# Where three tiles' tap products stand in TensorE's order, and x's third and fourth tile in two transfers

## The chip, the cores and the metric

The kernel runs on one core of one Trainium2 chip. A core has five engines that each take their instructions in order: TensorE (PE in the profile, with its weight loads as PEld), VectorE (DVE), ScalarE (ACT), GpSimd (POOL) and SyncE (SP, which here only issues transfers). They wait for each other and for transfers through semaphores. The metric is device microseconds of one execution, lower is better.

## The reference

Two layers on x of 512 tokens by 1024 channels, float32. Layer 0 is a convolution module and a gated feed-forward part, layer 1 is sliding-window attention and another feed-forward part, and an RMS norm ends it. Only the head of layer 0 matters here:

```python
def rmsnorm(x, g):
    xf = x.astype(jnp.float32)
    xf = xf * lax.rsqrt(jnp.mean(xf * xf, axis=-1, keepdims=True) + EPS)
    return (xf * g.astype(jnp.float32)).astype(x.dtype)

def conformer_conv(x, w_pw1, b_pw1, w_dw, b_dw, ln_g, ln_b, w_pw2, b_pw2):
    a = jax.nn.glu(x @ w_pw1 + b_pw1, axis=-1)
    y = lax.conv_general_dilated(                # 31 causal taps, each channel for itself
        a, w_dw[:, None, :].astype(a.dtype), window_strides=(1,),
        padding=((CONV_WIDTH - 1, 0),), dimension_numbers=('NWC', 'WIO', 'NWC'),
        feature_group_count=D_MODEL) + b_dw
    y = jax.nn.silu(layernorm(y, ln_g, ln_b))
    return y @ w_pw2 + b_pw2
...
h = h + conformer_conv(rmsnorm(h, norm_mix[l]), ...)
h = h + swiglu_ffn(rmsnorm(h, norm_ffn[l]), ffn_w_up[l], ffn_w_down[l])
```

## The kernel before

Channels lie on the 128 partitions and tokens along the row, so x is eight tiles of 128 by 512 (`h[0]` to `h[7]`), loaded by `load_x` (L376). Every float32 product is taken apart into a rounded high part and the rest, and costs three matmuls (`mm3`, `mm3_in_turn`, L339): high by high, high by rest, rest by high. ACT rounds the high part, DVE subtracts it. Weights come as chunks of 128 by 1024; `advance` (L252) loads six chunks ahead and splits three ahead.

**The start.** `load_x(0, 1)`, `load_x(1, 2)`, the rest of the first weight chunk, `load_x(2, 4)`, the second chunk, `load_x(4, 6)`, `load_x(6, 8)` and the taps' table are issued by SP in that order (L379 to L386); ACT issues three small transfers beside them. The loop at L705 splits the x tiles in order, on ACT and on DVE, with the first two weight chunks in pieces between them; on DVE it also lays out the tables of tap weights behind tiles 1 and 3 (L715). Both orders are written out by hand (`acts`, `dves`). Then both engines form the sum of squares for the norm.

**The first stage** handles the eight channel tiles `ct` of the convolution one after the other (`Conv`, L735, loop at L945):

- `project`: two halves of eight steps; a step is one `mm3_in_turn`, so a projection is 48 matmuls. They fill two banks, `gt` (the gate's argument) and `lin`. In the second half, for every tile but the first, the four steps for `gt` come first and then the four for `lin`. After each step it calls `inside(ct)` with the half and the number of the step.
- `begin`: `gate` multiplies both by the norm's factor, takes the sigmoid, and writes the gated tile `apad` (DVE L766, L768, L769 with ACT L767 between). Then SP writes `apad` to DRAM (`rowsd`) and reads it back four times, shifted, into `shifted`, one read for each quarter of the partitions (L775, L777). `products` makes some taps on ACT (L822) with sums on POOL (L824); `taps` makes others on DVE, one instruction for each tap.
- `rounds` makes 12 to 20 of the 31 taps on TensorE, from `shifted` and the tables, into a bank of its own: three, four or five rounds of four 32-column matmuls (the trace records each as two). It needs all four shifted reads.
- `last` (DVE L841) adds that bank to the tile's other taps.

TensorE's order is a chain (`in_turn`, L335): whatever is called first runs first, and what waits holds all that follows. The other engines' order is laid out by the framework's planner when the kernel is built, in which a line called earlier goes ahead if its inputs are ready; only the chains `tapped`, `copies`, `acts` and `dves` are fixed. The program's transfers share eight landing semaphores in rotation, so a transfer is issued once the one eight places before it has landed.

The rounds of a tile are called by `inside` of a later projection: those of tile 0 at the end of projection 2 (L927), those of tiles 1, 2 and 3 inside projections 3, 4 and 5 (L930 to L932), those of tiles 4 to 6 behind projection 7 (L949), and those of tile 7 last, in two halves, for the layer norm's means (L960). At the end of projection 3 stands a small table product, of projection 4 `shift_rows`, of projections 5 and 6 `sums` of the finished tiles and their squares. Then come the layer norm, the second pointwise product, and the two layers' other parts, all on the same TensorE.

Of the kernel before, what the change touches and what calls it, by code (L numbers as in the profile page):

```python
# [21 lines left out]
KT = D // P  # L22
# [150 lines left out]
def hybrid_trunk(ctx: ExitStack, tc: tile.TileContext, xT, W, prm_in, wdw_in, rnd_in, sinks, relb, onehot, fin, out):  # L173
# [87 lines left out]
    def split_chunk(i):  # L261
        r = block(i) if PLAN[i][0] == "prod" else raws.pop(i)
        stream["split"] = i + 1
        hi = wpool.tile([P, 1024], F32R, tag="whi", name=uid("whi"))
        lo = wpool.tile([P, 1024], F32R, tag="wlo", name=uid("wlo"))
        with ExitStack() as hold:
            for ins in held[0]:
                hold.enter_context(tc.issue_after(ins))
            done = (nc.scalar.copy(hi, r).ins, lo_engine[0].tensor_sub(lo, r, f32(hi)).ins)  # L269
        splits[i] = (hi, lo)  # L270
        return done
# [104 lines left out]
    def load_x(a, b):  # L376
        nc.sync.dma_start(hT[:, a:b, :], xT[a:b].rearrange("k p s -> p k s"))
# [1 line left out]
    load_x(0, 1)  # L379
    load_x(1, 2)  # L380
    nc.sync.dma_start(early[0][0][:, 256:1024], W[0][:, 256:1024])
    load_x(2, 4)
    nc.sync.dma_start(early[1][0], W[1])
    load_x(4, 6)
    load_x(6, 8)
# [257 lines left out]
    with conv_stage:  # L643
# [15 lines left out]
        def table():  # L659
            pf = bank()  # L660
            fs = temp()[0:NH, 0:3 * P]
            nc.tensor.matmul(pf[0:NH, 0:3 * P], lhs, oh, start=True, stop=True)
            nc.scalar.mul(fs, pf[0:NH, 0:3 * P], -1.0)
            nc.scalar.mul(sk, sk, -1.0)
            nc.sync.dma_start(f1.rearrange("o (h k) -> (o h) k", h=NH), fs)

        def table_rows():
            nc.sync.dma_start(fd.rearrange("q h k -> q (h k)"), f1.to_broadcast([16, NH * 3 * P]))
# [28 lines left out]
        def round_weights(cts, after=None):  # L697
            for ct in cts:
                at, n = ROUND_COLS[ct], 4 * ROUNDS[ct]
                with tc.issue_after(after) if after is not None else nullcontext():  # L700
                    after = nc.vector.tensor_mul(weights_of[ct], eye.unsqueeze(1).to_broadcast([P, n, 32]),
                                                 rnd[:, at:at + n].unsqueeze(2).to_broadcast([P, n, 32])).ins
            return after
# [145 lines left out]
        def shift_rows():  # L849

            b = bank()
            for e in range(2):
                in_turn(b, ones_m, y[e], start=e == 0, stop=e == 1)
            nc.scalar.mul(shift, b, -1.0 / 256)
            for t in y[0:2]:
                nc.vector.tensor_add(t, t, shift)
            nc.gpsimd.tensor_add(y[2], y[2], shift)

        def sums(*cts):

            if st[0] is None:
                st[0] = bank()
            src = []
            for i in cts:
                sq = next_of(1, sqs)
                nc.scalar.square(sq, y[i])
                src += [y[i], sq]
            for n, t in enumerate(src):
                in_turn(st[0][n * 32:(n + 1) * 32, :], ones32, t, start=cts[0] == 0, stop=cts[0] == KT - 2 - n // 2 * 2)
# [44 lines left out]
        def inside(ct):  # L914
            def at(half, n):
                if ct == 1 and (half, n) == (0, 5):
                    rms0.step1()
                    round_weights((0, 1, 2, 3), rms0.had)
                if ct == 1 and (half, n) == (1, 1):
                    rms0.step2()  # L920
                    convs[0].gate()
                    split_limit[0] = 2 * KT
                    held[0] = (convs[0].gated,)
                    held[0] = (split_chunk(5)[1],)
                    convs[0].products()
                    convs[0].taps()
                if half == 1 and n == 7 and ct == 2:  # L927
                    convs[0].rounds()
                    convs[0].last()
                if half == 0 and n == 7 and 3 <= ct < KT - 2:  # L930
                    convs[ct - 2].rounds()
                    convs[ct - 2].last()  # L932
                if half == 1 and n == 7:
                    if ct == 3:
                        table()
                    if ct == 4:
                        table_rows()
                    if ct == 4:
                        shift_rows()
                    if ct in (5, 6):  # L940
                        sums(2 * ct - 10, 2 * ct - 9)
            return at
# [370 lines left out]
```

## Time and profile before

| what | value |
|---|---|
| median of 3 runs | 1056.72 us (1055.94 to 1058.72) |
| the profiled execution | 1053.6 us, its span 1051.8 us |
| granted TensorE clock, mean | 0.999 |
| DVE, ACT, POOL busy | 754.4 us (72%), 501.4 us (48%), 184.5 us (18%) |
| first stage, from the first product to the layer norm | about 5 to 147 us of the span |

The span runs from the first to the last instruction; the execution's time has 1.8 us around it. Times inside the profile are microseconds from the start of the span. In a timeline row stand start, duration, engine, line, operation, output and inputs, the number of instructions merged, and in brackets how long the engine stood idle before it and what ended that. A releaser is inferred from what ended last, so it can name a bystander. In the answer for a tile, "DMA to landing" is the time from a transfer's issue until its data is there.

### The profile page before, as it was taken

The page shows a single profiled execution, that of the slowest core. Times are in us where ns is not written, and L with a number is a line of the kernel's source. Part 1 is how long each engine was busy: PE and PEld are TensorE (multiplying, and loading weights), DVE is VectorE, ACT ScalarE, POOL GpSimd, SP SyncE. Part 2 cuts the span into 40 slices and gives each one's busy share as a digit, 9 for nine tenths or more (in the row PEclk, how much of TensorE's full clock was granted, in tenths as well). Part 3 has the DMA queues.
Part 4 walks back from the last instruction along what each step waited for, and adds up shares of the span by engine and source line. Part 5 has one row for each costly group of instructions (what it writes and reads, how often), then busy time and mean ns, then how long its engine had stood idle before and what let it go on. Part 6 is the DMA issues. An engine that isn't in the chain of part 4 may idle for free.

```text
span 1051.8 us, 16099 instructions
## 1 busy us (share of the span) xinstructions
PE 1037.6 (99%) x6492; PEld 899.4 (86%) x6492; DVE 754.4 (72%) x981; ACT 501.4 (48%) x765; POOL 184.5 (18%) x200
## 2 busy tenths in 40 slices
PE   9999999999999999999999999999999999999997
PEld 7666568888998999899879878788899988998996
DVE  8799857599776587576684677578977754776663
ACT  6666645352552355155453766345355432542443
POOL 0799801311000000000130534041100000000000
PEclk9999999999999999999999999999999999999999
DMA  7656675324244124221323120232323431342112
GB/s 256 179 160 180 148 139 120 100 80 141 81 124 138 63 98 160 61 81 62 120 81 100 61 61 22 80 105 87 131 98 105 140 118 41 109 145 88 41 61 80
DMA packets 36918, 111.64 MB, mean 106 GB/s; under 512 B 4395, under 2 KB 7260, under 8 KB 36828
## 3 DMA queue, kind: packets, MB, share of 16 engines
q1 hardware_dynamic: 35692, 109.32, 35.0%
q10 hardware_dynamic: 1152, 1.29, 0.4%
q8 instruction: 51, 0.84, 0.3%
q14 instruction: 23, 0.19, 0.1%
HBM read 106.25 MB, written 4.73 MB: 106 GB/s over the span
## 4 chain that ended last, share of the span: by engine, by line
PE 88%; DVE 2%; issue 1%; ACT 1%; POOL 0%; POOLq 0%; ACTq 0%
PE bank L346 23%; PE bank L345 23%; PE bank L347 23%; PE bank L337 18%; PE bank L1242 2%; DVE quad L459 1%; DVE wlo L269 1%; ACT whi L269 0%; PE bank L450 0%; PE bank L1232 0%; PE bank L433 0%; DVE h L488 0%; DVE quad L280 0%; POOL rr L908 0%; ACT tmp L280 0%
## 5 line engine op out<-in xcount | busy, mean ns | idle before, releaser
L346 PE MATMUL bank<-quad,whi 128*128 128x256 f32 (+1 forms) x1536 | 488.5, 320 | 1.3 <-DVE quad L459 0.9
L345 PE MATMUL bank<-quad,whi 128*128 128x256 f32 (+1 forms) x1536 | 483.9, 320 | 0.3 <-ACT tmp L606 0.3
L347 PE MATMUL bank<-quad,wlo 128*128 128x256 f32 (+1 forms) x1536 | 482.6, 320 | 0.0
L269 ACT CAST whi<-raw 128x1024 fp32r<-128x1024 f32 x174 | 182.5, 1050 | 294.8 <-PE bank L346 197.4
L346 PEld LDWEIGHTS bank<-quad,whi 128*128 128x128 f32 x1536 | 292.6, 190 | 22.8 <-DVE quad L459 1.3
L345 PEld LDWEIGHTS bank<-quad,whi 128*128 128x128 f32 x1536 | 291.3, 190 | 23.0 <-ACT quad L280 0.7
L347 PEld LDWEIGHTS bank<-quad,wlo 128*128 128x128 f32 x1536 | 290.0, 190 | 20.2
L269 DVE TENSOR_TENSOR wlo<-raw,whi 128x1024 fp32r<-128x1024 f32 x174 | 220.5, 1270 | 112.4 <-ACT whi L269 110.1
L337 PE MATMUL bank<-quad,whi 128*128 128x512 f32 x512 | 160.9, 395 | 0.6 <-ACT whi L280 0.6
L337 PEld LDWEIGHTS bank<-quad,whi 128*128 128x128 f32 x512 | 94.8, 188 | 26.7 <-issue 4.0
L269 DVE TENSOR_TENSOR wlo<-blocks,whi 128x1024 fp32r<-128x1024 f32 x54 | 65.5, 1221 | 57.5 <-ACT whi L269 57.5
L269 ACT CAST whi<-blocks 128x1024 fp32r<-128x1024 f32 x54 | 56.6, 1048 | 91.7 <-PE bank L346 69.4
L337 PE MATMUL bank<-quad,wlo 128*128 128x512 f32 x256 | 99.9, 390 | 0.1
L824 POOL TENSOR_TENSOR quad<-quad 128x512 f32<-128x512 f32 x53 | 76.4, 1442 | 10.9 <-ACT quad L822 7.8
L337 PEld LDWEIGHTS bank<-quad,wlo 128*128 128x128 f32 x256 | 48.1, 188 | 10.7 <-DVE wlo L280 0.4
L1253 POOL TENSOR_TENSOR rs<-ss,mhalf 128x1 f32<-128x1 f32 x4 | 2.2, 549 | 298.0 <-DVE ss L1251 298.0
L423 POOL TENSOR_TENSOR tmp<-tmp,tmp 128x512 f32<-128x512 f32 x21 | 32.9, 1568 | 111.8 <-ACT tmp L421 100.5
L1115 POOL COPY sc<-sk 128x4 f32<-128x4 f32 x16 | 3.6, 256 | 257.1 <-DVE wlo L269 254.9
L822 ACT ACTIVATE quad<-apad,wdw 128x512 f32<-128x512 f32 x53 | 36.7, 718 | 17.8 <-POOL quad L824 17.8
L1139 POOL TENSOR_SCALAR sc<-sc,sm 128x256 f32<-128x256 f32 (+1 forms) x64 | 31.8, 518 | 65.9 <-DVE sm L1137 62.6
L488 DVE TENSOR_TENSOR h<-bank,h 128x512 f32<-128x512 f32 x56 | 37.1, 683 | 8.6 <-PE bank L347 8.5
L1135 ACT ACTIVATE sc<-sc,m 128x257 f32<-128x257 f32 (+1 forms) x64 | 30.2, 475 | 22.5 <-DVE m L1126 22.5
(168 smaller groups left out, 1010.5 us busy)
## 6 DMA issues: line engine op xcount, KB each, us to landing
raw<-in_W_dram SPq DMA_DIRECT2D x139, 512.0 KB, 3.6
blocks<-in_W_dram SPq DMA_DIRECT2D x36, 512.0 KB, 4.4
shifted<-rowsd SPq DMA_DIRECT2D x16, 262.0 KB, 5.4
shifted<-rowsd SPq DMA_DIRECT2D x12, 260.0 KB, 5.2
rowsd<-apad SPq DMA_DIRECT2D x8, 271.0 KB, 3.3
bias<-fd SPq DMA_DIRECT2D x8, 256.0 KB, 10.3
h<-in_xT_dram SPq DMA_DIRECT2D x3, 512.0 KB, 6.7
shifted<-rowsd SPq DMA_DIRECT2D x4, 264.0 KB, 4.8
```

The costliest lines, as they stand in the source:

```text
L269: done = (nc.scalar.copy(hi, r).ins, lo_engine[0].tensor_sub(lo, r, f32(hi)).ins)
L337: turn[0] = nc.tensor.matmul(*args, **kw).ins
L345: nc.tensor.matmul(out, w[0], x[0], start=start, stop=False, **kw)
L346: nc.tensor.matmul(out, w[0], x[1], start=False, stop=False, **kw)
L347: nc.tensor.matmul(out, w[1], x[0], start=False, stop=stop, **kw)
L423: eng.tensor_add(sq, self.acc[eng], sq)
L488: nc.vector.tensor_add(t, banks[m], t)
L822: nc.scalar.mul(pr, src, self.tap(j))
L824: nc.gpsimd.tensor_add(to, acc, pr)
L1135: nc.scalar.activation(sc[:, j, 0:1 + w], sc[:, j, 0:1 + w], AF.Exp, bias=self.m4[:, j:j + 1], scale=-1.0, accum_out=sm[:, j:j + 1])
L1139: nc.gpsimd.tensor_scalar(sc[:, j, 1:1 + w], sc[:, j, 1:1 + w], sm[:, j:j + 1], 0.0, op0=ALU.mult, op1=ALU.add)
L1242: nc.tensor.matmul(self.banks[g], x, w[:, k, :], start=False, stop=kp == LAST[1] - 1 and k == 1 and n == 2)
```

## The change

```diff
@@ -379,7 +379,8 @@
     load_x(0, 1)
     load_x(1, 2)
     nc.sync.dma_start(early[0][0][:, 256:1024], W[0][:, 256:1024])
-    load_x(2, 4)
+    load_x(2, 3)
+    load_x(3, 4)
     nc.sync.dma_start(early[1][0], W[1])
     load_x(4, 6)
     load_x(6, 8)
@@ -927,7 +928,7 @@
                 if half == 1 and n == 7 and ct == 2:
                     convs[0].rounds()
                     convs[0].last()
-                if half == 0 and n == 7 and 3 <= ct < KT - 2:
+                if (half, n) == (1, 3) and 3 <= ct < KT - 2:
                     convs[ct - 2].rounds()
                     convs[ct - 2].last()
                 if half == 1 and n == 7:
```

Inside projections 3, 4 and 5 the rounds and the add of tiles 1, 2 and 3 are called after the fourth step of the second half instead of after the eighth of the first: four steps later, between the steps for `gt` and those for `lin`. x's tiles 2 and 3 come in two transfers of 256 KB instead of one of 512 KB, so SP issues one transfer more, and all later ones move on by one in the rotation of the landing semaphores. Nothing else differs; no amount of arithmetic changes.

## The prediction

> **What bounds the kernel now.** I read the page's span first, then the groups of TensorE's matmuls from 24 to 146 us, kept apart by shape.
>
> ```profile
> span 1051.8 us, 16099 instructions
> ```
>
> ```profile
> L337 PE MATMUL bank<-shifted,tables 128*32 128x512 f32 x200 | 22.5, 594 | 3.4 <-DVE wlo L269 1.9 <-DMA shifted<-rowsd 0.8 <-issue 0.7
> ```
>
> All 3.4 us that TensorE idles ahead of rounds stand there, in three pieces under three names. TensorE's timeline gives their places: two steps of a projection, then the rounds of tiles 1, 2 and 3.
>
> ```profile
> 48.60 0.62 PE L337 MATMUL bank<-quad,whi 128*128 128x512 f32 x2
> ...
> 49.28 0.62 PE L337 MATMUL bank<-quad,whi 128*128 128x512 f32 x2
> ...
> 50.79 3.64 PE L337 MATMUL bank<-shifted,tables 128*32 128x512 f32 x32 [0.67 <-issue]
> ...
> 67.36 2.78 PE L337 MATMUL bank<-shifted,tables 128*32 128x512 f32 x24 [0.84 <-DMA shifted<-rowsd]
> ...
> 84.89 3.64 PE L337 MATMUL bank<-shifted,tables 128*32 128x512 f32 x32 [1.85 <-DVE wlo L269]
> ```
>
> A step costs 49.28 - 48.60 = 0.68. TensorE reached the three rounds at 50.12, 66.52 and 83.04 (start less idle) and began 0.67, 0.84 and 1.85 later. The names "issue" and "wlo" explain nothing: a split of weights is no input of a round. So I asked for the shifted rows' landings, tile by tile.
>
> ```profile
> L280 SPq DMA_DIRECT2D shifted<-rowsd x4: 319/423/1667, 42.7 to 44.0; - x4
> DMA to landing us min/median/max: 5.0/6.2/6.6
> ...
> L280 SPq DMA_DIRECT2D shifted<-rowsd x4: 319/426/430, 59.1 to 60.4; - x4
> DMA to landing us min/median/max: 4.5/5.8/6.8
> ...
> L280 SPq DMA_DIRECT2D shifted<-rowsd x4: 318/427/431, 77.7 to 79.0; - x4
> DMA to landing us min/median/max: 3.3/4.6/5.7
> ```
>
> Taking the longest time for the last issue: 44.0 + 6.6 = 50.6, 60.4 + 6.8 = 67.2, 79.0 + 5.7 = 84.7. Each stands 0.2 before the start of its rounds. All three waits are for shifted reads. Then comes the chain that ended last, and two stretches of the windows view (columns: PE, PEld, DVE, ACT, POOL).
>
> ```profile
> 84.89 56.94 PE bank L337 x382
> ```
>
> ```profile
> 52.20:124.40 72.20, 69.51 (x378) 45.58 (x373) 68.18 (x79) 48.65 (x73) 67.89 (x50) 1.00 0.63 162
> ...
> 134.00:1051.00 917.00, 908.69 (x5824) 810.68 (x5816) 639.10 (x831) 416.94 (x639) 91.06 (x117) 1.00 0.31 94
> ```
>
> From 84.89 to 141.8 the chain never leaves TensorE, and from 134 to the end it is busy 908.69 of 917.00. So what TensorE wins before 84.89 reaches the end, unless something later in the stage is not ready for an earlier TensorE. DVE is busy 68.18 of 72.20 from 52.2 to 124.4: it makes gates and taps at its own pace behind TensorE, and so sets when tiles' rows go out.
>
> **The move of the rounds.** Nothing is added or removed: the same matmuls, adds and transfers, with four steps (4 x 0.68 = 2.72) now ahead of the rounds.
>
> Tile 1: TensorE comes at 50.12 + 2.72 = 52.84, the rows at 50.6. The 0.67 goes.
> Tile 2: 66.52 - 0.67 + 2.72 = 68.57 against 67.2. The 0.84 goes; TensorE is 1.51 ahead.
> Tile 3: 83.04 - 1.51 + 2.72 = 84.25 against 84.7. It still waits and starts at 84.89, but with four steps left in the half instead of eight. It is now 2.72 ahead (3.36 of waits less the 0.64 that stays).
>
> Queued behind the rounds are now the steps for `lin`; they end where they would have, only without the waits. Behind `last` in DVE's queue stand the next gate's operations. I cost the three adds at nothing, since they come long after their rounds:
>
> ```profile
> 66.52 0.68 DVE L841 TENSOR_TENSOR quad<-bank,quad 128x512 f32<-128x512 f32 x1
> ```
>
> This is tile 1's add, whose rounds ended at 54.43: 12 us of cover, of which the move takes about 2. Without the cover each add would hold DVE for as long as it comes early. What is late next? I walked forward with TensorE 2.72 early, and looked at each thing that it takes from others: the squares for `sums`, and the rows of tiles 6 and 7.
>
> ```profile
> 101.46 0.63 ACT L866 ACTIVATE quad<-quad 128x512 f32<-128x512 f32 x1 [0.39 <-POOL quad L843]
> ```
>
> ```profile
> 106.23 1.06 PE L337 MATMUL bank<-quad,ones_m 128*32 128x512 f32 x8
> ...
> 118.34 6.21 PE L337 MATMUL bank<-shifted,tables 128*32 128x512 f32 x56
> ...
> 133.60 0.59 PE L337 MATMUL bank<-shifted,tables 128*32 128x256 f32 x4
> ```
>
> ```profile
> 123.95 0.13 PEld L337 LDWEIGHTS bank<-shifted,tables 128*32 128x32 f32 x4 [0.30 <-DVE quad L280]
> ```
>
> ```profile
> L280 SPq DMA_DIRECT2D shifted<-rowsd x4: 303/424/430, 114.7 to 116.0; - x4
> DMA to landing us min/median/max: 3.4/5.1/5.7
> ...
> L280 SPq DMA_DIRECT2D shifted<-rowsd x4: 303/424/430, 123.8 to 125.1; - x4
> DMA to landing us min/median/max: 3.4/4.8/5.6
> ```
>
> Squares: ready at 102.09, needed at 106.23 - 2.72 = 103.51. Fine.
> Tile 6: the 56 records from 118.34 are those of tiles 4 and 5 (24 + 32); the weight load at 123.95 is the first of tile 6. It would come at 121.23, but its rows land at 116.0 + 5.7 = 121.7, so at 121.9 with the 0.2 from landing to start. **A new wait of 0.67 takes the place of part of the old ones**, and 123.95 - 121.9 = 2.05 is left.
> Tile 7: 133.60 - 2.05 = 131.55 against 125.1 + 5.6 + 0.2 = 130.9. Fine, by 0.65.
>
> Tile 6's rows don't come earlier by themselves, since DVE writes its gated tile:
>
> ```profile
> 111.14 0.75 DVE L769 SCALAR_TENSOR_TENSOR apad<-bank,prm,tmp 128x512 f32<-128x512 f32 x1 [0.19 <-ACT tmp L767]
> ```
>
> The only idle time there is 0.19 for the sigmoid. What no trace of before shows is how the planner lays out DVE's queue anew. Bounds: `gt` is now done before the rounds, so the gate's first product can go ahead of `last` and hide 0.19 in each of three gates, 0.6 earlier; the other end is the longest stall in DVE's queue, 4.69 (below). I take 0, which is nearest to an order that stays.
>
> **x in two transfers.** This is one SP issue more. The start in the timelines of SP, ACT, DVE and PE, a row of SP's waits, and the landings of x's tiles 2 to 5 and of the second weight chunk:
>
> ```profile
> 2.59 0.47 SPq L383 DMA_DIRECT2D raw<-in_W_dram  x1
> 3.79 0.89 SPq L377 DMA_DIRECT2D h<-in_xT_dram  x2
> ```
>
> ```profile
> SPq L377 <- DMA prm<-in_prm_dram: 0.7, 1, 0.7
> ```
>
> ```profile
> 7.89 0.72 ACT L280 ACTIVATE quad<-h,prm 128x512 fp32r<-128x512 f32 x1 [1.55 <-DMA h<-in_xT_dram]
> ```
>
> ```profile
> 7.03 1.75 DVE L701 TENSOR_TENSOR tables<-eye,rnd 128x384 f32<-128x384 f32 x3
> ...
> 9.37 0.68 DVE L280 TENSOR_TENSOR wlo<-raw,whi 128x512 fp32r<-128x512 f32 x1
> ```
>
> ```profile
> 10.11 0.50 PE L337 MATMUL bank<-quad,wlo 128*128 128x512 f32 x1
> ```
>
> ```profile
> L377 SPq DMA_DIRECT2D h<-in_xT_dram x2: 378/408/437, 2.1 to 3.8; - x2
> DMA to landing us min/median/max: 5.8/6.2/6.7
> ```
>
> ```profile
> L383 SPq DMA_DIRECT2D raw<-in_W_dram x1: 468/468/468, 2.6 to 2.6; - x1
> DMA to landing us min/median/max: 6.6/6.6/6.6
> ```
>
> Tiles 2 and 3 land at 7.9, the second chunk at 9.2, tiles 4 and 5 at 10.5: 512 KB each 1.3, back to back. Tile 2 alone would land some 0.65 sooner, and ACT's 1.55 at 7.89 shrinks by that. But DVE is at the tables until 8.78 in a fixed order, and its split that ends at 10.05 releases TensorE's product at 10.11: no gain there. On the cost side the second chunk becomes the ninth transfer and takes over the wait for `prm`, so it is issued at 3.79 instead of 2.59, still over 4 us before its turn in the stream of data. Ends: nothing and one issue, 0.47, on everything behind. I take 0.
>
> [...]
>
> **The sum.** 0.67 + 0.84 + 1.85 - 0.64 - 0.67 = 2.05. The profiled execution of 1053.6 becomes 1051.5. The median of the runs is 3.1 above it, and I move it by the same amount: 1056.7 - 2.05 = **1054.7**. That is 0.19%; below 0.3%, here 3.2 us, a measurement of this kernel can't tell a change from none.
>
> **Rivals.**
>
> *Larger gain (24%).* If DVE's queue closes up by the 0.6 above, tile 6's rows come 0.6 sooner and the gain is 2.7; if tile 3's rows do too, it goes to 3.3: 1053.4 to 1054.0. For it: `gt` is ready sooner. Against it: DVE's pace is mostly taps and splits.
>
> *A bank takes the wait's place (9%).* Rounds need a free bank. If tile 2's get one that only the gate of tile 3 sets free, they begin at 71.6:
>
> ```profile
> 70.83 0.74 DVE L769 SCALAR_TENSOR_TENSOR apad<-bank,prm,tmp 128x512 f32<-128x512 f32 x1
> ```
>
> That is 3.0 behind 68.57; TensorE comes to tile 3 at 83.04 + 1.5 + 2.72 = 87.3 and is 84.89 + 2.72 - 87.3 = 0.3 ahead: 1056.4. Against it: none of the three waits now is for a bank.
>
> *The split of x costs (7%).* [...]
>
> *Slower (12%).* The new order of DVE's queue puts a weight split ahead of a gate, where it waits for ACT's rounding, as it does now at
>
> ```profile
> 52.24 2.08 DVE L269 TENSOR_TENSOR wlo<-raw,whi 128x1024 fp32r<-128x1024 f32 x1 [4.69 <-ACT whi L269]
> ```
>
> A second stall of 4.69 before tile 6's gate would land its rows at 126.6 instead of 121.9, against 123.95 before: 2.6 slower, 1059.3. It decides from 2.05 on; less only eats the gain. Against it: DVE had run out of taps there, and all its idle time from 52.2 to 124.4 is 4.0.
>
> That the rounds don't move can't be: their order on TensorE is a chain.
>
> **Chances and range.** My forecast has 48%. Faster by over 0.3% takes half of the larger gain (0.12) and a fifth of the forecast's own case (0.10, since three runs spread over 2.8): 0.22. Slower by over 0.3% needs the stall and some more, half of that case: 0.06. Between them 0.72. The range leaves out most of the slower case and the tail of the larger: 1052.7 to 1057.2.
>
> **What would show it.** Right: rounds of tiles 1 and 2 with no idle before them, tile 3's still starting near 84.9 with half a microsecond idle, the `sums` now at 106.23 near 103.5, and tile 6's first load near 121.9 with a wait of some 0.6. Wrong: idle before tile 2's rounds that ends with a DVE gate (the bank), x's tile 4 reaching ACT after 10.5 (the split), tile 6's gate after 111.9 or an idle DVE before it (the queue), or no wait at tile 6 (larger).

## The result, and the profile after

The kernel with the change took 1053.42 us (median of 7 executions, 1052.67 to 1054.40) beside 1056.56 us for the kernel before (7, 1055.41 to 1058.72): ratio 0.9969, 95% interval 0.9957 to 0.9980. A second comparison later, with 11 and 35 executions, gave 1054.42 beside 1055.75, ratio 0.9986 (0.9976 to 0.9995). So the size is not settled by one comparison. Over both, with 12 more executions of the kernel before from the first experiment, the means are 1056.30 (54) and 1053.96 (18): **2.3 us faster, 0.2%**. The forecast was 1054.7, a gain of 2.05.

And yet the two profiled executions, 1053.60 before and 1053.42 after, are nearly equal. Both things need explaining. First the lines of the page and of the groups (24 to 146 us) that answer to those of before:

```profile
span 1051.6 us, 16101 instructions
```

```profile
L337 PE MATMUL bank<-shifted,tables 128*32 128x512 f32 x200 | 22.5, 594 | 0.8 <-DMA shifted<-rowsd 0.8
```

TensorE's idle time ahead of rounds fell from 3.4 to 0.8. Its timeline: the rounds of tiles 0, 1, 2, 3, the `sums` of tiles 0 and 1 and of tiles 2 and 3, the rounds of tiles 4 to 6 and half of tile 7's:

```profile
42.74 2.78 PE L337 MATMUL bank<-shifted,tables 128*32 128x512 f32 x24 [0.84 <-DMA shifted<-rowsd]
...
53.88 3.64 PE L337 MATMUL bank<-shifted,tables 128*32 128x512 f32 x32
...
69.54 2.78 PE L337 MATMUL bank<-shifted,tables 128*32 128x512 f32 x24
...
85.14 3.64 PE L337 MATMUL bank<-shifted,tables 128*32 128x512 f32 x32
...
91.66 1.06 PE L337 MATMUL bank<-quad,ones_m 128*32 128x512 f32 x8
...
103.76 2.46 PE L337 MATMUL bank<-quad,ones_m 128*32 128x512 f32 x8
...
117.27 9.65 PE L337 MATMUL bank<-shifted,tables 128*32 128x512 f32 x88
...
132.92 2.60 PE L337 MATMUL bank<-shifted,tables 128*32 128x256 f32 x40
```

The three waits are gone. `sums(0, 1)` starts at 91.66; before, it was

```profile
94.13 1.06 PE L337 MATMUL bank<-quad,ones_m 128*32 128x512 f32 x8
```

But `sums(2, 3)` lasts 2.46 where it lasted 1.06, and by tile 4's rounds only 118.34 - 117.27 = 1.07 is left. The profile names the cause on ScalarE (its square of y3) and GpSimd:

```profile
104.49 0.63 ACT L867 ACTIVATE quad<-quad 128x512 f32<-128x512 f32 x1 [3.81 <-POOL quad L844]
```

```profile
100.44 2.32 POOL L838 TENSOR_TENSOR quad<-quad,quad 128x512 f32<-128x512 f32 x1
102.73 1.73 POOL L844 TENSOR_TENSOR quad<-quad,quad 128x512 f32<-128x512 f32 x1
```

GpSimd before, the same two adds:

```profile
100.12 1.30 POOL L843 TENSOR_TENSOR quad<-quad,quad 128x512 f32<-128x512 f32 x1
101.38 2.29 POOL L837 TENSOR_TENSOR quad<-quad,quad 128x512 f32<-128x512 f32 x1
```

**The planner swapped them.** L843 before is L844 after, the shift of y3 in `last`; L837 is L838, tile 4's add of its products in `taps`. Called later, the shift now goes behind, the square waits 3.81 for it, and ScalarE's products for tile 5 and the gates behind them are late. Tile 6's gate:

```profile
112.17 0.75 DVE L770 SCALAR_TENSOR_TENSOR apad<-bank,prm,tmp 128x512 f32<-128x512 f32 x1 [2.11 <-ACT tmp L768]
```

The rest is in the windows view. First the whole stretches of the prediction (PE, PEld, DVE, ACT, POOL busy, then the granted clock), then 6.8 us of the layer norm (PE busy, granted clock, DMA share, GB/s):

```profile
52.20:124.40 72.20, 72.20 (x390) 45.19 (x392) 64.60 (x76) 47.12 (x70) 66.25 (x48) 1.00 0.63 162
134.00:1051.00 917.00, 908.81 (x5810) 811.30 (x5801) 639.05 (x832) 417.52 (x638) 90.95 (x117) 1.00 0.31 95
```

```profile
141.00:144.40 3.40, 2.54 (x18) 1.00 0.23 51
144.40:147.80 3.40, 3.40 (x11) 0.51 1.16 125
```

TensorE, busy 69.51 of 72.20 us before, now counts as busy throughout; the 1.40 that `sums(2, 3)` loses stands inside its row and is counted too. Then, from 144.4 to 147.8, it runs at half the clock (0.51). Before's profile has no such stretch there:

```profile
144.00:146.00 2.00, 1.66 (x15) 1.00 0.70 130
146.00:148.00 2.00, 2.00 (x8) 1.00 1.14 114
```

It takes back the last microsecond: the second pointwise product starts at 148.08, at 147.96 before.

### The profile page after: what moved, and what is told of

Its sections match the earlier page's. It is cut to its first block, busy times and chain, and to the rows that moved or that the text cites. A ratio compares the mean times of both kernels' runs of the same rounds, so it can differ in the third digit from the quotient of the medians.

```text
span 1051.6 us, 16101 instructions
## 1 busy us (share of the span) xinstructions
PE 1039.6 (99%) x6492; PEld 899.9 (86%) x6492; DVE 754.5 (72%) x981; ACT 502.7 (48%) x765; POOL 185.7 (18%) x200
## 4 chain that ended last, share of the span: by engine, by line
PE 94%; DVE 2%; DMA 2%; issue 1%; ACT 1%; SPq 0%; POOL 0%; POOLq 0%; ACTq 0%; DVEq 0%
PE bank L337 23%; PE bank L345 23%; PE bank L346 23%; PE bank L347 23%; PE bank L1243 2%; DMA shifted<-rowsd 1%; DVE quad L460 1%; DMA h<-in_xT_dram 0%; DVE wlo L269 0%; DMA rowsd<-apad 0%; PE bank L451 0%; PE bank L1233 0%; PE bank L434 0%; ACT whi L269 0%; DVE h L489 0%
## 5 line engine op out<-in xcount | busy, mean ns | idle before, releaser
L269 ACT CAST whi<-raw 128x1024 fp32r<-128x1024 f32 x174 | 183.0, 1053 | 293.6 <-PE bank L346 197.4
```

## The experiments

Each kernel was compared with the kernel before on the same chip. "Clock" is the mean over executions of the granted TensorE clock.

| run | kernel | n | median us | ratio (95%) | clock | kernel before in that comparison |
|---|---|---|---|---|---|---|
| e1 | before, again | 12 | 1057.04 | 1.0012 (1.0002 to 1.0023) | 0.9957 | 1055.75, clock 0.9968 (35) |
| e2 | rounds only | 11 | 1053.92 | 0.9981 (0.9972 to 0.9991) | 0.9977 | same |
| e3 | split of x only | 12 | 1057.20 | 1.0007 (0.9995 to 1.0019) | 0.9963 | same |
| e4 | the change, again | 11 | 1054.42 | 0.9986 (0.9976 to 0.9995) | 0.9971 | same |
| e5 | GpSimd's order | 8 | 1052.19 | 0.9967 (0.9954 to 0.9979) | 0.9980 | 1055.83, clock 0.9965 (31) |
| e6 | before, 3 fillers at tile 3 | 12 | 1055.57 | 0.9996 (0.9985 to 1.0006) | 0.9979 | same |
| e7 | tiles 1 and 2 only | 12 | 1056.88 | 1.0014 (1.0004 to 1.0023) | 0.9954 | same |
| e8 | fillers at the layer norm | 12 | 1053.21 | 0.9975 (0.9965 to 0.9984) | 0.9992 | same |
| e9 | tile 3 only | 11 | 1053.96 | 0.9979 (0.9969 to 0.9990) | 0.9971 | 1056.06, clock 0.9969 (21) |
| e10 | before, 2 fillers at tile 3 | 11 | 1054.96 | 0.9990 (0.9981 to 0.9999) | 0.9977 | same |
| e11 | rounds, GpSimd's order, fillers | 5 | 1052.34 | 0.9962 (0.9950 to 0.9975) | 0.9986 | same |
| e12 | e11, tile 3 later | 5 | 1053.01 | 0.9962 (0.9947 to 0.9977) | 0.9990 | same |

e1 sets the scale: the same program comes out at 1.0012, and the interval excludes 1. Differences of a tenth of a per cent between such ratios prove nothing by themselves; the verdicts below rest on traces and clocks as well.

### The kernel before, again (e1)

No edit.

> The kernel before, once more, as a second look at it. The first profile of it shows 3.36 us of idle TensorE ahead of the rounds of tiles 1, 2 and 3 (0.67 + 0.84 + 1.85) and none ahead of tile 0's. Theory A (the waits are as in that one profile): again 3.1 to 3.7 us ahead of tiles 1 to 3 and nothing ahead of tile 0, the ones_m matmuls of shift_rows near 94.1 us and the first matmul of sums(2, 3) near 106.2, and a profiled execution near 1053.6. Theory B (single pieces of the shifted rows land up to some 2 us later in some executions, and the rounds at mid projection have nothing in hand for it): the idle of the four tiles differs from the first profile by over 0.7 us in sum, with a shifted read of over 6.9 us to landing behind it, and the profiled execution lies nearer the median of 1056.6. Theory C (the difference of the medians comes from behind 150 us, from the granted clock for instance): the first 150 us are as in the first profile and the extra time stands behind them. Ratio 1.000 within 0.002 under each.

Tiles 1, 2 and 3 in this profile:

```profile
50.94 3.64 PE L337 MATMUL bank<-shifted,tables 128*32 128x512 f32 x32 [0.51 <-issue]
...
67.01 2.78 PE L337 MATMUL bank<-shifted,tables 128*32 128x512 f32 x24 [0.34 <-DVE quad L280]
...
85.14 5.34 PE L337 MATMUL bank<-shifted,tables 128*32 128x512 f32 x32 [2.47 <-DVE wlo L269]
```

The waits are 0.51 + 0.34 + 2.47 = 3.32, against 3.36 in the first profile: theory A holds for the sum, and theory B falls: the slowest shifted reads of tiles 0 to 3 took 6.4, 6.4, 6.5 and 5.9 us (tile 0's fourth read has no landing in the trace). The matmuls near 94.1 that I had named for `shift_rows` are those of `sums(0, 1)`. But this execution took 1058.00, and tile 3's rounds lasted 5.34 in place of 3.64. The windows view (PE busy, granted clock, DMA share, GB/s), in narrow strips around three stretches:

```profile
82.10:85.50 3.40, 0.93 (x7) 1.00 1.03 278
85.50:85.60 0.10, 0.10 (x5) 0.59 1.06 412
85.60:88.90 3.30, 3.30 (x20) 0.50 0.75 200
88.90:89.00 0.10, 0.10 (x5) 0.84 0.89 125
...
146.90:147.00 0.10, 0.00 (x0) 0.80 0.74 205
147.00:150.30 3.30, 3.15 (x10) 0.50 1.15 143
...
556.50:556.60 0.10, 0.10 (x3) 0.80 0.00 0
556.60:559.90 3.30, 3.30 (x18) 0.50 0.73 199
```

A strip at 0.59 has run 0.82 of its length at half clock, so the first stretch goes from 85.52 to 88.93: 3.41 us. Half of it, 1.71, is lost to a busy TensorE; tile 3's rounds took 5.34 - 3.64 = 1.70 longer. The others start at 146.96 and 556.56, so 61.44 and 409.60 behind each other, which is 18 and 120 lengths of 3.413 each. In e7 two stretches start at 86.31 and 147.75, again 61.44 apart, in e4 at 144.35 and 553.95, again 409.60. **Within each of these three executions the half clocks fit a grid of 3.413 us.** It doesn't start with the program: counted back to the start of the span, it stands at 0.19 in e1, 0.98 in e7 and 0.99 in e4 (and at 1.09 and 0.47 by the one stretch each of the change's first profile and e2). That it goes on where no stretch marks it is an estimate from these distances. Ahead of e1's first half clock TensorE was idle for 3.40 - 0.93 = 2.47 of 3.40 us.

So theory C was right that the clock makes the difference, and wrong that it all stands behind 150 us.

### The change in its two halves (e2, e3), and again (e4)

e2 is the second hunk of the diff alone, e3 the first.

> Only the rounds of tiles 1 to 3 are moved; x's tiles three and four stay in one transfer. If the rounds carry the whole change: ratio 0.996 to 0.998, the changed kernel's 0.997, or 0.1 to 0.2 us better, since the second weight chunk is issued at 2.59 us again and not at 4.07, and the steps at the start run 0.1 to 0.2 us earlier. The rival, that the split of x brings a part of the gain: ratio 0.9985 or more. In the trace no idle ahead of the rounds of tiles 1, 2 and 3, and ScalarE's square of y3 waits about 3.8 us for GpSimd's shift of y3, as in the changed kernel.

> Only x's third and fourth tile go in two transfers; the rounds stand where they stood. By the prediction 0, by the changed kernel's trace 0.1 to 0.2 us slower: ratio 1.000 to 1.0005. Rival of the prediction (the split brings gain): 0.999 or less. The waits ahead of the rounds of tiles 1 to 3 stay, 3 us or more together.

> The changed kernel once more. Ratio 0.996 to 0.998 as before. Theory A: the same 0.84 us ahead of tile 0's rounds and none ahead of tiles 1 to 3. Theory B: the wait ahead of tile 0's rounds comes and goes from execution to execution (0 to 1 us), and none stands ahead of tiles 1 to 3, since they have about 2.7 us in hand. ScalarE's wait of 3.8 us for the shift of y3 stands again, since it comes from the order on GpSimd's queue, which is the program's. If the granted clock's dip at 142 to 149 us (0.50 in one stretch) is chance, it is gone or has another place; if it belongs to the change, it is there again.

e2 is as fast as the change (its ratio is 0.0005 below e4's, inside the noise of e1). e3 is the kernel before, within the interval. Both ratios of the moved rounds, 0.9981 and 0.9986, lie just above the 0.996 to 0.998 that I expected. In seven profiles with x's tiles together, TensorE comes to tile 0's rounds (start less idle) at 42.13 on average, in seven with the split at 42.19, and the seven of each spread over 0.87 and 0.96: **no effect of the split shows**, and the 0.1 to 0.2 us that I read from the first two profiles are well inside that spread. e3 keeps its waits:

```profile
51.08 3.64 PE L337 MATMUL bank<-shifted,tables 128*32 128x512 f32 x32 [0.35 <-DMA shifted<-rowsd]
68.47 2.78 PE L337 MATMUL bank<-shifted,tables 128*32 128x512 f32 x24 [1.64 <-DVE quad L842]
...
85.91 3.64 PE L337 MATMUL bank<-shifted,tables 128*32 128x512 f32 x32 [1.79 <-DMA shifted<-rowsd]
```

In e4 tiles 0 to 2 have no idle, so the wait at tile 0 belonged to that execution. Tile 3's rounds have some, as in e2 (1.11), against both expectations; the 2.7 us in hand that I had named is not there:

```profile
86.19 3.64 PE L337 MATMUL bank<-shifted,tables 128*32 128x512 f32 x32 [1.37 <-DMA shifted<-rowsd]
```

Start to start, these profiles agree well once they are measured from the moment at which TensorE comes to tile 0's rounds. One half-clock stretch at tile 3 is taken off e1 (1.71).

| from tile 0's rounds to | before, e1, e3 | after, e4, e2 | gain of the means |
|---|---|---|---|
| `sums(0, 1)` | 52.47, 52.43, 52.88 | 49.76, 50.32, 50.08 | 2.54 |
| tile 4's rounds | 76.68, 76.64, 77.10 | 75.37, 75.38, 75.40 | 1.43 |

So the waits give 2.54, and 1.11 of it is lost again between the two. ScalarE's square waits 3.83 in e4 and 3.82 in e2, as in the first profile. The half clock at the layer norm came again in both (144.4, 143.9).

### GpSimd's order put back (e5)

```
 taps:   -                nc.gpsimd.tensor_add(y[ct], y[ct], self.acc)
         +                if ct != 4:
         +                    nc.gpsimd.tensor_add(y[ct], y[ct], self.acc)
 last:   -                    nc.gpsimd.tensor_add(y[ct], y[ct], shift)
         +                    shifted = nc.gpsimd.tensor_add(y[ct], y[ct], shift).ins
         +                    with tc.issue_after(shifted):
         +                        nc.gpsimd.tensor_add(y[4], y[4], convs[4].acc)
```

> The changed kernel, with GpSimd's two adds near 100 to 103 us in the order of the kernel before: y3's shift first, then the add of tile 4's products. Every other queue is as in the changed kernel. Theory 1 (the order on GpSimd's queue gives back about 1.1 us of what the rounds won): ScalarE's square of y3 waits 0.4 us or so and not 3.8, the eight matmuls of sums(2, 3) take 1.06 us and not 1.9 to 2.5, tile 4's rounds start 1.0 to 1.4 us after 12.1 us less than now stands between sums(0, 1) and them (24.2 us from sums(0, 1) to tile 4's rounds as in the kernel before, against 25.1 to 25.6 in the changed one), and the median lies 0.9 to 1.4 us under the changed kernel's. Theory 2 (the 1.1 us come back in another way, since tile 6 waits for its rows at 121.9 and loads at the same time): the square's wait goes, but tile 6's first load still stands near 122.9 and the median stays within 0.4 us of the changed kernel's. Both leave the granted clock alone: half-clock windows of 3.4 us near 144 and 554 us in some executions, as before.

GpSimd's two adds, then TensorE's `sums(2, 3)` and tile 4's rounds:

```profile
101.19 1.29 POOL L845 TENSOR_TENSOR quad<-quad,quad 128x512 f32<-128x512 f32 x1
102.43 2.29 POOL L847 TENSOR_TENSOR quad<-quad,quad 128x512 f32<-128x512 f32 x1
```

```profile
104.61 1.07 PE L337 MATMUL bank<-quad,ones_m 128*32 128x512 f32 x8
...
116.72 9.65 PE L337 MATMUL bank<-shifted,tables 128*32 128x512 f32 x88
```

From `sums(0, 1)` at 92.50 to 116.72 are 24.22 us, as in the kernel before (24.21) and not 25.06 to 25.61. From tile 0's rounds to tile 4's: 74.00, a gain of 2.81 over the kernel before. Theory 1 holds: **the order of two adds on GpSimd cost 0.85 to 1.40 us** (25.06, 25.32 and 25.61, less 24.21). The ratio, 0.9967 beside 0.9986 in e4 and 0.9969 in the first comparison, allows that and shows no more. At like clocks (0.997 and 0.998) e5's executions average 1052.38 (4), those of the change 1053.81 (8), in other series of runs: 1.43 less.

### Tiles 1 and 2 alone (e7), tile 3 alone (e9)

```
 e7:  +                if (half, n) == ((0, 7) if ct == 5 else (1, 3)) and 3 <= ct < KT - 2:
 e9:  +                if (half, n) == ((1, 3) if ct == 5 else (0, 7)) and 3 <= ct < KT - 2:
```

> The rounds of tiles 1 and 2 move, tile 3's stay at mid projection; x's split as in the change. GpSimd keeps the order of the kernel before. By the prediction's steps: no idle ahead of tiles 1 and 2, so TensorE comes to tile 3's rounds 1.5 us earlier and waits there for rows that land as late as before, 2.5 to 3.4 us and not 1.85: the gain of the first two is given back at the third, sums(0, 1) near 94 to 95 us, ratio 0.999 to 1.001. By theory C the longer idle brings the half clock at 86 to 92 us in more executions than in the kernel before: ratio 1.000 to 1.002, mean granted clock no higher than that of the kernel before. If each wait counted by itself: 1.5 us faster, ratio 0.9986.

> Only tile 3's rounds move to three quarters of the projection; those of tiles 1 and 2 stay in the middle; x's split as in the change. If the gain is made at tile 3 alone (what tiles 1 and 2 win comes back as a longer wait at tile 3, as e7 showed): idle of 0.3 to 1.7 us ahead of tiles 1 and 2 each, none or under 0.3 us ahead of tile 3's, sums(0, 1) within 0.5 us of the changed kernel's 91.7 to 92.7, no half clock between 84 and 92 us, and the median within 0.5 us of the changed kernel's. If the moves add up: 1 to 1.5 us slower than the changed kernel. GpSimd's two adds stand in the changed kernel's order, so ScalarE's wait of 2 to 4 us for y3's shift is there too.

Tiles 1, 2 and 3 in e7, then in e9 with `sums(0, 1)`:

```profile
53.46 3.64 PE L337 MATMUL bank<-shifted,tables 128*32 128x512 f32 x32
69.12 2.78 PE L337 MATMUL bank<-shifted,tables 128*32 128x512 f32 x24
85.55 5.34 PE L337 MATMUL bank<-shifted,tables 128*32 128x512 f32 x32 [3.49 <-DMA shifted<-rowsd]
```

```profile
50.95 3.64 PE L337 MATMUL bank<-shifted,tables 128*32 128x512 f32 x32 [0.73 <-DMA shifted<-rowsd]
66.89 2.78 PE L337 MATMUL bank<-shifted,tables 128*32 128x512 f32 x24 [0.21 <-issue]
85.24 3.64 PE L337 MATMUL bank<-shifted,tables 128*32 128x512 f32 x32
91.75 1.06 PE L337 MATMUL bank<-quad,ones_m 128*32 128x512 f32 x8
```

In e7 TensorE gains at tiles 1 and 2 and stands 3.49 at tile 3, for rows that come no sooner: nothing is won (52.43 to `sums(0, 1)` without the half clock, 52.59 on average before). And the longer idle brings the half clock: 5.34 for the rounds, the lowest mean clock of all kernels, and a median 1 us above the kernel before's. e9 leaves the first two waits and has the gain (50.00). **It is made at tile 3 alone.**

### Keeping TensorE busy without removing the wait (e6, e10)

```
 e6:  +                if self.ct == 3:
      +                    for _ in range(3):
      +                        in_turn(c, ones_m, self.a[:, 0:S], start=True, stop=True, skip_group_check=True)
 e10: the same with range(2)
```

The fillers write into the bank that the rounds then overwrite.

> The kernel before, with three matmuls of 0.47 us each put ahead of tile 3's rounds, into the bank that the rounds overwrite: the wait for tile 3's rows stays as long as it is, but TensorE works through most of it. Theory C (a part of the kernel before's time is the granted clock, halved for 3.4 us in some executions after the idle 1.8 to 2.5 us ahead of tile 3's rounds, 1.7 us each time): no half clock between 84 and 92 us, the mean granted clock of the executions rises by 0.0005 to 0.0015 over that of the kernel before of the same call, and the median falls by 0.3 to 1 us. Rival (the clock has no part in it, only the waits count): the same median within 0.3 us, or some 0.1 to 0.4 us slower where the fillers end after the rows have landed, and the same mean clock.

> As e6 with two fillers in place of three. The trace of e6 showed that each of these matmuls is two passes of 0.46 us: three of them last 2.74 us, longer than the wait, and delayed the rounds; two last 1.83 us and end when the rows land. Theory C: no half clock between 84 and 92 us, mean granted clock of the executions 0.001 over that of the kernel before of this call, and without e6's delay the median is 0.6 to 1.4 us under that of the kernel before, with the wait for tile 3's rows as long as ever. Rival: the median stays within 0.3 us.

e10's fillers and tile 3's rounds:

```profile
83.08 1.88 PE L337 MATMUL bank<-apad,ones_m 128*128 128x512 f32 x4
85.75 3.64 PE L337 MATMUL bank<-shifted,tables 128*32 128x512 f32 x32 [0.79 <-issue]
```

The wait is as long as ever (the rounds start at 85.75), but no half clock follows it, in e6 either. Both mean clocks rise, by 0.0014 in e6 and 0.0008 in e10. e10's median is 1.1 below the kernel before's, though it reaches tile 4's rounds as late as a kernel before without half clock (76.67): what it gains is clock, not wait. e6's three fillers, twice as long as I had sized them, put tile 4's rounds 0.8 later (77.57, against 76.81 on average in before, e1 and e3), and little is left of the gain: here the rival's time came true, though not its reason. Both fillers also brought the swap on GpSimd (ScalarE's square waits 2.73 and 2.75), but `sums(2, 3)` takes 1.07 as before, so it costs nothing there. The effect of e10 rests on an interval that just excludes 1; the clocks and traces carry more than the ratio.

### The layer norm's pause (e8)

```
 for half in range(2):  ...
 +            if half:
 +                idle(1)
 scales:                pm = spread(mv, in_turn)
 +            idle(1)
```

> The changed kernel, with one matmul of 0.47 us put into each of two pauses of the layer norm, near 140.8 (0.52 us idle) and 143.8 us (0.34 us idle). Theory C (idle TensorE in a window of 3.4 us halves the clock in the next one): no half clock near 144 to 148 us, or in fewer executions; the mean granted clock rises by 0.0005 to 0.0015 over the changed kernel's 0.9971 to 0.9981, and the median falls by 0.5 to 1.2 us, less 0.1 to 0.2 us where a filler overruns its pause. Rival (the few columns of the small matmuls count as work, or two fillers are too little): the half clock stays, and the time is the changed kernel's or 0.1 to 0.3 us worse.

```profile
141.00:144.40 3.40, 3.15 (x20) 1.00 0.22 41
144.40:147.80 3.40, 3.40 (x15) 1.00 1.17 127
```

No half clock, and the mean clock is 0.9992, the highest of all. (Behind the last matmul a half clock starts at 1050.20. The grid carried back from there has a window at 142.25 to 145.67; TensorE is idle for 0.25 of it and busy for 3.16.) Of the eleven profiles without these fillers seven have a half clock between 143 and 152; of the three with them (e8, e11, e12) none. Each filler is two passes and 0.86 to 1.02 us, which is more than its pause: from the last join to the second pointwise product it is 7.13 us, 6.84 in a kernel without half clock (before, e5). With the half clock it was 8.03, 7.88 and 7.76 (after, e4, e2). So 0.3 is paid each time to save 0.9 to 1.2 where the half clock would have come. By the ratios, 0.9975 and e4's 0.9986, it wins about a microsecond, and that is a comparison across two series of runs.

### Put together (e11, e12)

e11 is the moved rounds, x in one transfer, e5's order and e8's fillers; e12 calls tile 3's rounds two steps later still:

```
 +                if (half, n) == ((1, 5) if ct == 5 else (1, 3)) and 3 <= ct < KT - 2:
```

> What the runs point to, put together: the rounds of the change, x unsplit, GpSimd's order of e5, the two layer norm fillers of e8. If the effects add: under the changed kernel by 1.3 us (GpSimd's order), 1 us (the clock at the layer norm) and 0.1 us (x unsplit), 2.2 to 2.6 us in sum, some 1051.2 to 1052.2 us, ratio 0.9945 to 0.996, mean granted clock 0.9985 to 0.9995. If e5's fewer half clocks were chance, or if its order and the fillers win the same time: 1052 to 1053.

> e11 with tile 3's rounds two more steps later, 1.36 us: the idle of 0 to 1.4 us (0.7 to 0.8 on average) that the changed kernel's traces still show ahead of them goes. By the waits: 0.5 to 0.9 us better than e11, no idle over 0.1 us ahead of tile 3, and the squares for sums(2, 3) still in time, since y3's shift moves by 0.6 us at most. Rival: tile 3's end goes late by as much (the wait comes back at sums(2, 3), whose slack is about 1.5 us), and the median is e11's within 0.3 us.

With five executions each, e11's median of 1052.34 lies just outside the 1051.2 to 1052.2 that I expected if the effects add, and inside the 1052 to 1053 of the alternative; it can't be told from e5: that the effects add is not shown. In e12 the idle ahead of tile 3 is gone, and tile 4's rounds come 1.68 earlier than in e11 (73.10 against 74.78 from tile 0's). But TensorE then stands at tile 6's first weight load:

```profile
122.03 0.19 PEld L337 LDWEIGHTS bank<-shifted,tables 128*32 128x32 f32 x8 [1.39 <-DVE bank L280]
```

0.30 of idle stands before each of the four loads ahead of it, so 1.09 is a wait, for tile 6's rows, the last of which land at 121.9. The rival had the wait come back too, but at `sums(2, 3)`, which here takes 1.07. At the second pointwise product e12 is 0.76 ahead of e11 (103.94 and 104.70 from tile 0's rounds), and its profiled execution lost that again to a half clock at 551. Neither median that I had named for e12 came: it is 0.67 above e11's, with five executions each that overlap. Both are 0.38% under the kernel before.

## Why the prediction was right, and where it was not

**The three waits.** Right: all three were for shifted reads. Their sum repeats (3.36, 3.32, 3.78 in before, e1, e3), their parts don't.

**The move.** Right: tiles 1 and 2 lose their waits in every profile of the change, and tile 3's rows set when TensorE goes on. I had 0.64 left of tile 3's wait; it was 0, 1.37 and 1.11. With 2.72 ahead as a forecast, 2.54 was measured at `sums(0, 1)`.

**DVE's adds cost nothing.** Right. Its queue did change as the larger-gain rival said: `gt`'s product (L767) goes ahead of `last` and hides 0.19 in two gates. That gain did not appear in the time.

**"Squares: ready at 102.09, needed at 103.51. Fine."** Wrong, and the step that failed. I took the time at which y3's shift was done before, and looked for a new order on DVE's queue only. The same freedom of the planner acted on GpSimd's queue, where it cost 1.11 in the change on average. The sign that I had written down for a trouble with the queue did come (tile 6's gate after 111.9, with idle ahead of it), and the slower rival had the right kind of mechanism on the wrong engine, at about a quarter of its price (1.11 for 4.7).

**Tile 6's wait of 0.67.** The place was right, but the change never reached it, since the lead was lost before: its first load stands at 122.88, without a wait. With GpSimd's order put back (e5) it is 0.16, and with more lead (e12) 1.09.

**x's split at nothing.** Right: TensorE comes to tile 0's rounds at 42.13 on average without it, at 42.19 with it. No run shows a cost in time of one transfer more (e3's ratio is 1.0007, 0.9995 to 1.0019), so the rival in which the split costs didn't come either.

**The step to the median.** I carried the gain over to a median 3.1 above the profiled execution and did not ask what those 3.1 were. They are largely half-clock windows: before's profile has none up to the last matmul, e1's has three. In the executions of the first four experiments' comparison (47 of the kernel before) and the 18 of the change (11 there, 7 of the first comparison), grouped by their granted clock:

| clock | before | after |
|---|---|---|
| 0.999 and more | 1054.31 (4) | 1052.89 (5) |
| 0.997 and 0.998 | 1055.34 (21) | 1053.81 (8) |
| 0.996 and less | 1057.43 (22) | 1055.27 (5) |

At the highest clock the change is worth 1054.31 - 1052.89 = 1.42, with few executions, and the traces give 1.43. (The last row is not like for like: before's goes down to 0.994, after's to 0.996.) The remaining 0.9 of the mean gain of 2.3 goes with the mean clock, 0.9965 before and 0.9975 after: 0.0010 of 1052 us is about 1 us of full speed. (That is rough: the mean clock also counts a low stretch behind the last matmul in some executions, as from 1050.54 to the end in before's profile, 0.50; no matmul runs in it.) e7 (3.49 idle at tile 3, mean clock 0.9954) and e6 and e10 (idle filled, 0.9979 and 0.9977), beside 0.9965 and 0.9969 for the kernel before, show that the wait at tile 3 brings such windows, so the move that shortens it removes them there. Whether it also makes those at the layer norm more or less frequent stays open. The limit of 0.3% that I had set for telling a change from none is borne out in part: the change's two ratios, 0.9969 and 0.9986, both exclude 1, but so does e1's 1.0012, for the same program.

So the sum of 2.05 met the mean of 2.3 by luck, through two errors that cancel: 2.05 of waits was 1.42 after GpSimd's queue had taken its part, and 0.9 came from a clock that the prediction did not know of.

## What to carry to other kernels

Where a planner lays out the queues, ask of every engine, and not only of the one that you watch, which two instructions near a moved call have no order between them; here the order of two adds on GpSimd took nearly half of what the waits gave. A wait removed ahead of one consumer is only won if the next one doesn't wait for data that come no sooner (tiles 1 and 2 here, with tile 3 behind them): find the last of the row, and move that. And before a gain of some tenths of a per cent is read from a pair of profiles or medians, look at each execution's granted clock, and compare at like clocks.

## What was not expected of the hardware

- The granted clock was 0.50 for stretches of 3.41 us (85.52 to 88.93 in e1), at a cost of up to 1.70 (tile 3's rounds, 5.34 in place of 3.64). Stretches of one execution start 61.44 or 409.60 apart (e1, e4, e7), which fits a grid of 3.413 us that doesn't start with the program (0.19, 0.99 and 0.98 from the start of the span). An execution can have none up to the last matmul (before, e5, e6, e8, e11) or three (e1). After an idle of 2.47 and 3.49 us ahead of tile 3's rounds the half clock came (e1, e7); after 1.85, 1.79 and 1.61 (before, e3, e11) it did not. Of these waits, 2.47 and 2.65 lay in the 3.41 us ahead of the half clock in e1 and e7, and 1.53 and 1.61 in one window of the grid in before and e11. (There the grid is an estimate, carried back from the half clock that starts behind the last matmul at 1050.54 and 1049.48.)
- Idle time by the profile isn't the only measure. At the layer norm 0.86 us of idle in a window (3.40 - 2.54) preceded a half clock; the matmuls there have 1 or 128 columns. The pauses stand at the same instructions in all eleven profiles without fillers there; TensorE is busy for 2.46 to 2.66 of the 3.41 us ahead of the seven half clocks. In two of the four without one, before and e5, the grid carried back from the tail gives 2.81 or more for each window there. So in these nine profiles the half clock goes with how the grid falls on the pauses. One filler matmul in each of two pauses (3.03 or more busy in every window there) came with no half clock in three profiles.
- The slowest of a tile's shifted reads takes 5.8 to 7.7 us to land for tile 0 and 6.5 to 7.5 for tile 2, over the fourteen profiles (for tile 0, of the three reads whose landing the trace has); ahead of tile 0's reads these kernels differ in nothing but the split of x. A wait of 0.84 at tile 0's rounds came in the change's first profile and in neither e4 nor e2.
- A matmul of 128x512 on f32 as issued here is recorded as two passes: e6's three fillers are six records in 2.74 us, e10's two are four in 1.88, so 0.43 for each record more. A filler costs twice what I took one matmul to last.
